# Longer leads in a hand-written issue order, a recurrence split into three chains, and a triangular inverse begun on 16x16 blocks

## The chip, the cores and the metric

One core of one Trainium2 chip runs the whole program. The metric is the time of one execution in microseconds (us). The kernel before took 1440.12, 1442.78 and 1443.78 us in three runs, so its median is 1442.78 us. The trace is of one further execution, which took 1445.36 us.

The engines are PE (TensorE, matrix products), DVE (VectorE), ACT (ScalarE), POOL (GpSimd) and SP (SyncE, which here only starts DMAs). PEld is the loading of weights into TensorE.

## What is computed

A transformer block on 512 tokens of width 1024: an input projection, differential attention with 8 heads, a gated delta rule with 8 key heads and 16 value heads, a gated merge, an MLP and a gated last branch. What matters here is the gated delta rule and the end of attention:

```
lower = tril(einsum(k_beta, k) * decay, -1)            # one 64x64 block per chunk and head
tmat  = triangular_solve(eye + lower, eye, lower=True, unit_diagonal=True)
u, w  = tmat @ v_beta, tmat @ (k_beta * exp(gc))
for each chunk:                                        # state is carried from chunk to chunk
    v_new = u_c - w_c @ state
    o_c   = (q_c * exp(gc)) @ state + intra_c @ v_new
    state = state * exp(g_last) + k_dec.T @ v_new
o_b = rmsnorm(o, gain) * silu(z)

w = softmax(s)                                         # attention, two softmaxes a head
o = rmsnorm((w[0] - lam * w[1]) @ v, gain)
```

Both kernels use chunks of 128 instead of 64, which is the same function. So each of the 8 key heads has 8 matrices of 128x128 to invert (2 value heads by 4 chunks).

## The kernel before

The program is one list of work for five engines. In the part that the change touches, the *mix stage*, PE runs two kinds of work. The *filler* is the input projection: 88 tiles, each of 24 matmuls of 128x512, whose weights arrive through SP (`raw<-w`, line 104), are split by ACT (113, 114) into a high part `whi` and a low part `wlo`, and completed by a DMA that POOL starts (115). The *chains* are the small dependent steps of a head: `gdn_a` (products of keys and queries, line 392), `gdn_i` (the inverse, 480), `gdn_b` (the rest of the delta rule, 504) and `attn` (650).

A planner writes PE's order while the program is built (lines 311 to 355). Each chain is a generator. Its `yield r` says that its next step may be put into the list when PE has been given r more microseconds of work, counted by a fixed price per matmul. Steps that are due go first; between them filler matmuls go in, two at a time. So `yield` sets how much filler lies between a PE step and the next step, which needs what DVE, ACT or a DMA makes of the first. If the number is smaller than what the other engines take, PE waits there, since PE and all other engines run their lists in order. The order on the other engines is set by the framework's scheduler from the same program.

The inverse is made in blocks. `gdn_i` writes the 32x32 diagonal blocks of `B` to DRAM (`ld_d`, line 462) and loads them back so that each of 128 partitions holds one matrix and a quarter of the columns (`L`, 486). DVE substitutes forward in 31 steps of two instructions (494, 495) into `Uq`. Four DMAs write `Uq` to DRAM (`ud_d`, 499) and four bring it back as the diagonal blocks of `U` (502). Then `gdn_b` transposes the blocks on DVE (512 to 514) and joins 32 to 64 and 64 to 128 by matmuls into `psY`, `psT`, `psU`, `ps6` and `ps7`. After that come the four chunks of the recurrence (550 to 605), the norm of the result on DVE (608 to 611), and its transposition into `psoT` (617). All of `gdn_b` of a head waits for `gdn_b` of the head before and for its gate tiles (line 737).

The lines that the prediction's steps touch most:

```
511   yield 8.0          # from the issue of the loads of U to the transposes
516   yield 3.0          # from the transposes to psY
612   yield 6.0          # from the norm of o to psoT
683   yield 5.0 + 0.5 * b    # from the weights of the softmax to psaT
702   yield 5.0          # from the norm of attention's output to psaoT
```

Of the kernel before, what the change touches and what calls it, by code (L numbers as in the profile page):

```python
# [17 lines left out]
T = 512  # L18
# [9 lines left out]
C_W = C_IDT + 256  # L28
# [8 lines left out]
def hybrid_block(ctx, tc, xT, pT, w1, wba, wa, wb, wo, wup, wdn, wple, wpg, vecs, rows, consts, out):  # L37
# [28 lines left out]
    idT = C[:, C_IDT:C_IDT + 256]  # L66
# [215 lines left out]
    ld_d = dram.tile([8, 32, 1024], F32, name="ld_d")  # L282
# [8 lines left out]
    Y6 = bp.tile([128, 8, 64], F32, name="Y6")  # L291
    Ubuf = [bp.tile([128, 8, 128], F32, name=f"U{i}") for i in range(2)]
    for t in (TT, TA, Yx, Y6, *Ubuf):
        G.memset(t, 0.0)

# [96 lines left out]
    def gdn_a(hk):  # L392
# [67 lines left out]
        for b in range(4):  # L460
            dst = ld_d[hk].rearrange("(e b) (r n) -> r b e n", b=4, r=32)[:, b]
            nc.sync.dma_start(dst, Bf[32 * b:32 * b + 32, :, 32 * b:32 * b + 32])
# [17 lines left out]
    def gdn_i(hk):  # L480
# [3 lines left out]
        L = gpool.tile([128, 32, 32], F32, name="L")  # L484
        for q in range(4):
            nc.sync.dma_start(L[32 * q:32 * q + 32].rearrange("p r n -> p (r n)"), ld_d[hk])
        Uq = gpool.tile([128, 8, 32], F32, name="Uq")
        tmp = gpool.tile([128, 256], F32, name="tmpq")
        V.tensor_copy(Uq.rearrange("p m r -> p (m r)"), idT)
        yield 8.0  # L490
        for j in range(31):
            m, r = j // 4 + 1, 31 - j
# [5 lines left out]
        for q in range(4):  # L498
            nc.sync.dma_start(ud_d[hk].rearrange("p (m q) n -> p q m n", q=4)[:, q], Uq[32 * q:32 * q + 32])  # L499
# [4 lines left out]
    def gdn_b(hk):  # L504

        d = st_.pop(hk)
        (kqh, kql), kt, vb, B, intra, U, r2, eq, edr = (d[n] for n in ("kqs", "kt", "vb", "B", "intra", "U", "r2", "eq", "edr"))
        Bf = B.rearrange("p i c n -> p (i c) n")
        U4 = U.rearrange("p e (k n) -> p e k n", k=4)
        b0, b1, b2, b3 = (slice(32 * i, 32 * i + 32) for i in range(4))  # L510
        yield 8.0
# [4 lines left out]
        yield 3.0  # L516
# [30 lines left out]
        o = [bp.tile([128, NC, 128], F32, name=f"o{i}") for i in range(2)]  # L547
        sso = bp.tile([128, 2, NC], F32, name="sso")
# [57 lines left out]

        rt = bp.tile([128, 2, NC], F32, name="rt")
# [4 lines left out]
        yield 6.0  # L612
# [37 lines left out]
    def attn(h):  # L650
# [9 lines left out]
        sso = apool.tile([128, NC], F32, name="asso")  # L660
        yield 1.5
        for b in range(NC):
# [15 lines left out]
            rr = apool.tile([128, 2], F32, name="rr", bufs=3)  # L678
            V.reciprocal(rr, st[:, 2:4])
# [37 lines left out]
    def units():  # L717
        for h in range(-1, 8):
            if h >= 0:
                yield gate_tile(h, 0)  # L720
                yield gate_tile(h, 1)
            if h == 7:
                for n in range(16):
                    yield branch_gate(n)
# [324 lines left out]
```

## Time and profile before

| | |
|---|---|
| the profiled execution | 1445.36 us, of which the span of the trace is 1443.4 us |
| median of three runs | 1442.78 us |
| PE busy | 1351.0 us, 94% of the span |
| DVE, ACT, POOL busy | 825.5, 655.1, 213.3 us |
| PE busy from 200 to 680 us | 439.00 of 480 us |
| PE busy from 800 us to the end | 617.61 of 643.4 us |

The mix stage lies from about 40 to 800 us. From 200 to 680 us the same pattern repeats once a head, about every 85 us. A matmul of 128x512 starts every 0.23 us when TensorE's granted clock is 1.00 (2.4 GHz) and every 0.43 us when it is 0.50 (1.2 GHz). A matmul in plain float32 of the small kind shows as two records in the trace, and as one row in the lists of instructions. "Idle" before an instruction is the time for which its engine had nothing to do, with what released it.

### The profile page before, as it was taken

The page shows a single profiled execution, that of the slowest core. Times are in us where ns is not written, and L with a number is a line of the kernel's source. Part 1 is how long each engine was busy: PE and PEld are TensorE (multiplying, and loading weights), DVE is VectorE, ACT ScalarE, POOL GpSimd, SP SyncE. Part 2 cuts the span into 40 slices and gives each one's busy share as a digit, 9 for nine tenths or more (in the row PEclk, how much of TensorE's full clock was granted, in tenths as well). Part 3 has the DMA queues.
Part 4 walks back from the last instruction along what each step waited for, and adds up shares of the span by engine and source line. Part 5 has one row for each costly group of instructions (what it writes and reads, how often), then busy time and mean ns, then how long its engine had stood idle before and what let it go on. Part 6 is the DMA issues. An engine that isn't in the chain of part 4 may idle for free.

```text
span 1443.4 us, 20586 instructions
## 1 busy us (share of the span) xinstructions
PE 1351.0 (94%) x7378; PEld 1104.5 (77%) x7378; DVE 825.5 (57%) x2324; ACT 655.1 (45%) x1322; POOL 213.3 (15%) x230
## 2 busy tenths in 40 slices
PE   6999999989998999898999999999999999999985
PEld 4777777868776777776877878888888888888985
DVE  6559585867958587694732353357443224433574
ACT  5656565655555565464645332254332223223241
POOL 3221111111111111111001000000421001210241
PEclk9999999999999999999999999999999999999998
DMA  7877656565565665656597863352123233233321
GB/s 233 192 185 171 142 137 148 149 154 139 142 144 124 154 147 140 146 125 133 142 243 191 234 220 117 116 167 83 49 91 97 93 92 98 89 102 102 110 81 59
DMA packets 93879, 197.73 MB, mean 137 GB/s; under 512 B 33713, under 2 KB 39217, under 8 KB 93777
## 3 DMA queue, kind: packets, MB, share of 16 engines
q1 hardware_dynamic: 81104, 150.28, 34.3%
q0 software_dynamic: 12672, 46.14, 17.0%
q8 instruction: 58, 0.95, 0.3%
q14 instruction: 45, 0.36, 0.1%
HBM read 133.40 MB, written 16.84 MB: 104 GB/s over the span
## 4 chain that ended last, share of the span: by engine, by line
PE 62%; DVE 17%; DMA 10%; issue 2%; ACT 2%; SPq 1%; POOL 0%; ACTq 0%; POOLq 0%; DVEq 0%
PE ps L78 52%; DVE acc L362 3%; DMA U<-ud_d 2%; PE psat L78 2%; DMA wlo<-raw 2%; DMA ud_d<-Uq 2%; DVE Uq L495 2%; DVE tmpq L494 1%; DMA ot<-ob_d 1%; DMA g_d<-gth 1%; DVE h L830 1%; PE psS L78 1%; SPq L499 1%; DVE ht L829 1%; PE psx L78 1%
## 5 line engine op out<-in xcount | busy, mean ns | idle before, releaser
L78 PE MATMUL ps<-u_hi,whi 128*128 128x512 f32 (+1 forms) x952 | 389.5, 410 | 1.0 <-DVE mr L889 1.0
L78 PE MATMUL ps<-u_lo,whi 128*128 128x512 f32 (+1 forms) x952 | 375.5, 395 | 0.0
L78 PE MATMUL ps<-u_hi,wlo 128*128 128x512 f32 (+1 forms) x952 | 254.0, 405 | 3.2 <-DMA wlo<-raw 3.2
L78 PEld LDWEIGHTS ps<-u_hi,whi 128*128 128x128 f32 x952 | 182.5, 192 | 41.9 <-issue 3.4
L78 PEld LDWEIGHTS ps<-u_hi,wlo 128*128 128x128 f32 x952 | 180.0, 195 | 44.0 <-DMA wlo<-raw 4.4
L78 PEld LDWEIGHTS ps<-u_lo,whi 128*128 128x128 f32 x952 | 181.8, 191 | 35.1
L96 ACT CAST whi<-raw 128x1024 fp32r<-128x1024 f32 (+1 forms) x93 | 92.3, 994 | 225.8 <-PE ps L78 220.1
L97 DVE TENSOR_TENSOR wlo<-raw,whi 128x1024 fp32r<-128x1024 f32 x83 | 101.2, 1220 | 108.0 <-PE ps L78 87.5
L115 POOL DMA_DIRECT2D wlo<-raw x88 | 76.2, 866 | 569.9 <-ACT wlo L114 368.0
L113 ACT CAST whi<-raw 128x1024 fp32r<-128x1024 f32 x88 | 92.1, 1046 | 80.1 <-PE ps L78 78.2
L114 ACT ACTIVATE wlo<-whi 128x1024 fp32r<-128x1024 f32 x88 | 92.6, 1052 | 0.0
L78 PE MATMUL ps<-hid_lo,whi 128*128 128x512 f32 x224 | 88.6, 395 | 0.0
L78 PE MATMUL ps<-hid_hi,whi 128*128 128x512 f32 x224 | 88.5, 395 | 0.0
L78 PE MATMUL ps<-brh,whi 128*128 128x512 f32 x208 | 82.4, 397 | 0.7 <-ACT whi L96 0.7
L78 PE MATMUL ps<-brl,whi 128*128 128x512 f32 x208 | 82.3, 396 | 0.0
L362 DVE SCALAR_TENSOR_TENSOR acc<-ps,cw,acc 128x511 f32<-128x511 f32 (+2 forms) x96 | 71.5, 744 | 12.3 <-ACT acc L359 11.9
L891 POOL TENSOR_TENSOR mr<-mr 128x512 f32<-128x512 f32 (+1 forms) x37 | 39.3, 1064 | 218.5 <-ACT hid_hi L890 218.4
L889 DVE SCALAR_TENSOR_TENSOR mr<-ps,r 128x512 f32<-128x512 f32 (+1 forms) x37 | 22.9, 619 | 74.1 <-PE ps L78 70.6
L78 PE MATMUL ps<-hid_hi,wlo 128*128 128x512 f32 x224 | 56.8, 395 | 0.0
L495 DVE TENSOR_TENSOR Uq<-Uq,tmpq 128x60 f32<-128x60 f32 (+24 forms) x248 | 52.4, 211 | 4.0
L494 DVE TENSOR_TENSOR tmpq<-L,Uq 128x60 f32<-128x60 f32 (+24 forms) x248 | 51.5, 207 | 3.4
L78 PE MATMUL ps<-brh,wlo 128*128 128x512 f32 x208 | 52.9, 396 | 0.0
(317 smaller groups left out, 2377.2 us busy)
## 6 DMA issues: line engine op xcount, KB each, us to landing
raw<-w SPq DMA_DIRECT2D x88, 512.0 KB, 3.8
wlo<-raw POOLq DMA_DIRECT2D x88, 512.0 KB, 5.3
raw<-wup SPq DMA_DIRECT2D x32, 512.0 KB, 3.5
raw<-wdn SPq DMA_DIRECT2D x32, 512.0 KB, 3.6
raw<-wb SPq DMA_DIRECT2D x16, 512.0 KB, 4.0
gB<-gcr_d SPq DMA_DIRECT2D x16, 256.0 KB, 4.2
bB<-ber_d SPq DMA_DIRECT2D x16, 256.0 KB, 4.8
L<-ld_d SPq DMA_DIRECT2D x32, 128.0 KB, 4.8
```

Of the source, the lines that this page charges most:

```text
L78: PE.matmul(ps, lhsT=lhsT, rhs=rhs, start=start, stop=stop, **k)
L96: S.copy(hi, src)
L97: (eng or V).tensor_tensor(lo, src, hi.bitcast(F32), op=sub)
L113: S.copy(whi, raw)
L114: S.activation(wlo, whi.bitcast(F32), AF.Copy, scale=-1.0)
L115: nc.gpsimd.dma_start(wlo, raw, accum_op=add)
L362: V.scalar_tensor_tensor(acc[:, s:], in0=ps[:, :T - s], scalar=cw[:, j, w:w + 1], in1=acc[:, s:], op0=mult, op1=add)
L494: V.tensor_tensor(tv, bc(L[:, j, j + 1:], [128, m, r], 1), bc(Uq[:, :m, j], [128, m, r], 2), op=mult)
L495: V.tensor_tensor(Uq[:, :m, j + 1:], Uq[:, :m, j + 1:], tv, op=sub)
L499: nc.sync.dma_start(ud_d[hk].rearrange("p (m q) n -> p q m n", q=4)[:, q], Uq[32 * q:32 * q + 32])
L889: V.scalar_tensor_tensor(r[:, :n], in0=ps[:, :n], scalar=0.0, in1=r2[:, sl], op0=mx, op1=mult)
L891: G.tensor_tensor(r[:, :n], r[:, :n], r[:, :n], op=mult)
```

## The change

The change does these things:

- The diagonal blocks that DVE inverts are 16x16. `ld_d` is written by 8 DMAs, `L` is loaded by 2 of 64 partitions, and the substitution has 15 steps of two instructions. A new first part of the chain joins 16 to 32 with two groups of 32 matmuls, `psY16` and `psU16`, which use all four groups of 32 columns in turn. It needs a transpose of each of the four 32-row groups of `U`, four scalings and four copies.
- `gdn_b` is split into `gdn_u` (inverse), `gdn_s` (recurrence) and `gdn_n` (norm and `psoT`), so that the three can be in different heads at once; only `gdn_n` waits for the gate tiles.
- Several leads are longer: 12.0 and 5.0 where 8.0 and 3.0 stood, 11.0 for 6.0 ahead of `psoT`, 6.0 + 0.5 b for 5.0 + 0.5 b ahead of `psaT`, 7.0 for 5.0 ahead of `psaoT`.
- Attention keeps its two softmaxes unnormalized and folds their sums into one factor and into the epsilon of the norm: one long DVE instruction a block goes, short ones on one column come.
- The filler's order in a head is key, query, values, then attention's three tiles, then the gates of the head before.
- Two DMAs fill `ud_d` with zeros at the start, since only its 16x16 blocks are written later.

```diff
...
-    ld_d = dram.tile([8, 32, 1024], F32, name="ld_d")
+    ld_d = dram.tile([8, 64, 256], F32, name="ld_d")
...
+    T3 = bp.tile([128, 8, 32], F32, name="T3")
+    Ye = bp.tile([128, 8, 2, 16], F32, name="Ye")
...
-    for t in (TT, TA, Yx, Y6, *Ubuf):
+    for t in (TT, TA, Yx, Y6, T3, Ye, *Ubuf):
...
+    for i in range(2):
+        nc.sync.dma_start(ud_d[4 * i:4 * i + 4].rearrange("h (p b) j n -> h p (b j n)", p=32).rearrange("h p n -> (h p) n"), Ubuf[i].rearrange("p e n -> p (e n)"))
...
-        for b in range(4):
-            dst = ld_d[hk].rearrange("(e b) (r n) -> r b e n", b=4, r=32)[:, b]
-            nc.sync.dma_start(dst, Bf[32 * b:32 * b + 32, :, 32 * b:32 * b + 32])
+        for b in range(8):
+            bs = slice(16 * b, 16 * b + 16)
+            dst = ld_d[hk].rearrange("(s e b) (r n) -> s b r e n", s=2, b=4, r=16)[b % 2, b // 2]
+            nc.sync.dma_start(dst, Bf[bs, :, bs])
...
-        L = gpool.tile([128, 32, 32], F32, name="L")
-        for q in range(4):
-            nc.sync.dma_start(L[32 * q:32 * q + 32].rearrange("p r n -> p (r n)"), ld_d[hk])
-        Uq = gpool.tile([128, 8, 32], F32, name="Uq")
-        tmp = gpool.tile([128, 256], F32, name="tmpq")
+        L = gpool.tile([128, 16, 16], F32, name="L")
+        for q in range(2):
+            nc.sync.dma_start(L[64 * q:64 * q + 64].rearrange("p r n -> p (r n)"), ld_d[hk])
+        Uq = gpool.tile([128, 8, 16], F32, name="Uq")
+        tmp = gpool.tile([128, 128], F32, name="tmpq")
...
-        for j in range(31):
-            m, r = j // 4 + 1, 31 - j
+        for j in range(15):
+            m, r = j // 2 + 1, 15 - j
...
-        for q in range(4):
-            nc.sync.dma_start(ud_d[hk].rearrange("p (m q) n -> p q m n", q=4)[:, q], Uq[32 * q:32 * q + 32])
+        for q in range(2):
+            for i in range(2):
+                h16, p = slice(16 * i, 16 * i + 16), 64 * q + 32 * i
+                nc.sync.dma_start(ud_d[hk][:, h16, h16].rearrange("p (m q) n -> p q m n", q=2)[:, q], Uq[p:p + 32])
...
-    def gdn_b(hk):
...
-        d = st_.pop(hk)
-        (kqh, kql), kt, vb, B, intra, U, r2, eq, edr = (d[n] for n in ("kqs", "kt", "vb", "B", "intra", "U", "r2", "eq", "edr"))
+    def gdn_u(hk):
...
+        B, U = (st_[hk][n] for n in "BU")
...
-        b0, b1, b2, b3 = (slice(32 * i, 32 * i + 32) for i in range(4))
-        yield 8.0
+        bq = b0, b1, b2, b3 = [slice(32 * i, 32 * i + 32) for i in range(4)]
+        yield 12.0
...
+        T16 = [TT[:, :, 0], TA[:, :, 1], TT[:, :, 1], T3]
+        for i in range(4):
+            V.transpose(T16[i][bq[i]], U4[bq[i], :, i])
+        Y16 = [Ye[:, :, 0], Yx[:, :, 0, :16], Ye[:, :, 1], Yx[:, :, 1, :16]]
+        yield 5.0
+        psY16 = pb.tile([128, 8, 16], F32, name="psY16", tag="b")
+        for e in range(8):
+            for i in range(4):
+                mm(psY16[bq[i], e], Bf[:, e, bq[i]], T16[i][:, e, :16])
+        for i in range(4):
+            if i % 2:
+                S.activation(Y16[i][bq[i]], psY16[bq[i]], AF.Copy, scale=nm16[bq[i]])
+            else:
+                V.tensor_scalar(Y16[i][bq[i]], psY16[bq[i]], nm16[bq[i]], None, op0=mult)
+        yield 2.0
+        psU16 = pb.tile([128, 8, 16], F32, name="psU16", tag="b")
+        for e in range(8):
+            for i in range(4):
+                mm(psU16[32 * i:32 * i + 16, e], Y16[i][:, e], U4[:, e, i, 16:])
+        for i in range(4):
+            (S.copy if i % 2 else V.tensor_copy)(U4[32 * i:32 * i + 16, :, i, 16:], psU16[32 * i:32 * i + 16])
+        yield 2.0
...
-        yield 3.0
+        yield 5.0
...
-        o = [bp.tile([128, NC, 128], F32, name=f"o{i}") for i in range(2)]
-        sso = bp.tile([128, 2, NC], F32, name="sso")
+    def gdn_s(hk):
...
+        d = st_[hk]
+        (kqh, kql), kt, vb, intra, U, r2, edr = (d[n] for n in ("kqs", "kt", "vb", "intra", "U", "r2", "edr"))
+        o = d["o"] = [bp.tile([128, NC, 128], F32, name=f"o{i}") for i in range(2)]
+        sso = d["sso"] = bp.tile([128, 2, NC], F32, name="sso")
...
+    def gdn_n(hk):
...
+        d = st_.pop(hk)
+        o, sso, eq = (d[n] for n in ("o", "sso", "eq"))
...
-        yield 6.0
+        yield 11.0
...
+        l2 = apool.tile([128, NC], F32, name="l2")
...
-            rr = apool.tile([128, 2], F32, name="rr", bufs=3)
-            V.reciprocal(rr, st[:, 2:4])
-            V.tensor_tensor(rr[:, 1:2], rr[:, 1:2], nlam, op=mult)
-            V.tensor_scalar(ws[1][:, :n], ws[1][:, :n], rr[:, 1:2], None, op0=mult)
-            V.scalar_tensor_tensor(ws[0][:, :n], in0=ws[0][:, :n], scalar=rr[:, 0:1], in1=ws[1][:, :n], op0=mult, op1=add)
-            yield 5.0 + 0.5 * b
...
+            rr = apool.tile([128, 1], F32, name="rr", bufs=3)
+            V.reciprocal(rr, st[:, 3:4])
+            V.scalar_tensor_tensor(rr, in0=rr, scalar=st[:, 2:3], in1=nlam, op0=mult, op1=mult)
+            V.tensor_scalar(l2[:, b:b + 1], st[:, 2:3], st[:, 2:3], EPS, op0=mult, op1=mult)
+            V.scalar_tensor_tensor(ws[0][:, :n], in0=ws[1][:, :n], scalar=rr, in1=ws[0][:, :n], op0=mult, op1=add)
+            yield 6.0 + 0.5 * b
...
-        V.tensor_scalar(sso, sso, 1.0 / 128.0, EPS, op0=mult, op1=add)
+        V.scalar_tensor_tensor(sso, in0=sso, scalar=1.0 / 128.0, in1=l2, op0=mult, op1=add)
...
-        yield 5.0
+        yield 7.0
...
     def units():
...
-            if h >= 0:
-                yield gate_tile(h, 0)
-                yield gate_tile(h, 1)
-            if h == 7:
-                for n in range(16):
-                    yield branch_gate(n)
-            else:
-                yield aq_tile(h + 1)
+            if h < 7:
...
+                yield aq_tile(h + 1)
...
-    done |= {(n, -1) for n in ("kq_read", "B_read", "k_read", "av_read", "B", "T", "A", "I")}
+            if h >= 0:
+                yield gate_tile(h, 0)
+                yield gate_tile(h, 1)
+        for n in range(16):
+            yield branch_gate(n)
...
+    done |= {(n, -1) for n in ("kq_read", "B_read", "k_read", "av_read", "B", "T", "A", "I", "U")}
...
-        chains.append([0.0, (("I", h), ("B", h - 1), ("Z", h, 1)), gdn_b, h, ("B", h)])
+        chains.append([0.0, (("Z", h, 1), ("S", h)), gdn_n, h, ("B", h)])
+        chains.append([0.0, (("U", h), ("B", h - 1)), gdn_s, h, ("S", h)])
+        chains.append([0.0, (("I", h), ("U", h - 1)), gdn_u, h, ("U", h)])
...
+    c[:, C_NM] = np.where(p % 32 >= 16, -1.0, 0.0)
```

On PE, at the place where the inverse of head 4 (counted from 0) reaches PE. Before, the last filler matmuls, then `psY` (the first join, 32x32), then attention's `psav`:

```order
L78 MATMUL ps<-u_hi,whi_5242 128x512
L78 MATMUL ps<-u_lo,whi_5242 128x512
L78 MATMUL psY<-TT,B 32x32 x16
L78 MATMUL psav<-C,vT 128x128 x4
L78 MATMUL ps<-u_hi,whi_5242 128x512
L78 MATMUL ps<-u_lo,whi_5242 128x512
```

Now, at the same place of the same head, `psY16` begins (its name is printed without the digits of the tile):

```order
L80 MATMUL ps<-u_hi,whi_5295 128x512
L80 MATMUL ps<-u_lo,whi_5295 128x512
L80 MATMUL psY_5363<-TT,B 32x16
L80 MATMUL psY_5363<-TA,B 32x16
L80 MATMUL psY_5363<-TT,B 32x16
L80 MATMUL psY_5363<-T_346,B 32x16
```

What stood as one block of 16 rows, two groups of columns in turn, now has 32 rows of four groups in turn ahead of it, with half the columns; `psU16` (32 rows of 16x16) follows 10 filler matmuls later, and the old `psY` after that.

On DVE, ahead of the instructions that normalize `o` (the inputs of `psoT`). Before, in head 3:

```order
L494 TENSOR_TENSOR tmpq<-L,Uq 128x75
L90 TENSOR_TENSOR nw_t<-rt 128x8
L698 TENSOR_SCALAR asso<-asso 128x4
L495 TENSOR_TENSOR Uq<-Uq,tmpq 128x5x15
L91 TENSOR_TENSOR nw_t<-nw_t,nw_h 128x8
L87 TENSOR_SCALAR art<-asso 128x4
L494 TENSOR_TENSOR tmpq<-L,Uq 128x70
L92 SCALAR_TENSOR_TENSOR rt<-nw_t,rt 128x8
L88 TENSOR_SCALAR nw_h<-asso 128x4
L495 TENSOR_TENSOR Uq<-Uq,tmpq 128x5x14
L611 TENSOR_TENSOR o_4545<-o_4545,rt 128x512
L611 TENSOR_TENSOR o_4546<-o_4546,rt 128x512
```

Now, in head 3:

```order
L94 SCALAR_TENSOR_TENSOR rt<-nw_t,rt 128x8
L92 TENSOR_TENSOR nw_t<-art 128x4
L92 TENSOR_TENSOR nw_t<-rt 128x8
L93 TENSOR_TENSOR nw_t<-nw_t,nw_h 128x4
L93 TENSOR_TENSOR nw_t<-nw_t,nw_h 128x8
L94 SCALAR_TENSOR_TENSOR art<-nw_t,art 128x4
L94 SCALAR_TENSOR_TENSOR rt<-nw_t,rt 128x8
L92 TENSOR_TENSOR nw_t<-art 128x4
L651 TENSOR_TENSOR o_4736<-o_4736,rt 128x512
L651 TENSOR_TENSOR o_4737<-o_4737,rt 128x512
```

The steps of the substitution (`tmpq`, `Uq`), which stood between the steps of the norm, are gone from here; only attention's norm (`art`) still alternates with it.

On SP, around the way of the inverse through DRAM. Before, in head 2:

```order
L104 DMA raw_3403<-w 128x1024
L499 DMA ud_d<-Uq 256x1x32 x4
L104 DMA raw_3552<-w 128x1024
L502 DMA U_346<-ud_d 32x8x32 x4
L104 DMA raw_3712<-w 128x1024
L104 DMA raw_3819<-w 128x1024
```

Now, in head 2:

```order
L106 DMA raw_3365<-w 128x1024
L509 DMA ud_d<-Uq 32x8x16 x4
L512 DMA U_348<-ud_d 32x8x32 x4
L106 DMA raw_3480<-w 128x1024
L750 DMA oa_d<-of 128x512
```

The load of weights that stood between the writes of `ud_d` and the loads of `U` now stands behind both in five of the eight heads, as here.

## Rows read from the trace of the kernel before

**Rows 1.** The page: span, then busy time of PE and DVE with share and instructions.
```profile
span 1443.4 us, 20586 instructions
PE 1351.0 (94%) x7378; PEld 1104.5 (77%) x7378; DVE 825.5 (57%) x2324; ACT 655.1 (45%) x1322; POOL 213.3 (15%) x230
```

**Rows 2.** Stretches (us): length, busy PE, PEld, DVE, ACT, POOL, PEclk (granted clock), DMA.
```profile
200.00:680.00 480.00, 439.00 (x2649) 350.89 (x2647) 342.39 (x1219) 271.68 (x635) 71.14 (x78) 0.96 0.60 141
680.00:800.00 120.00, 113.02 (x648) 91.70 (x649) 55.05 (x203) 64.44 (x134) 12.92 (x15) 1.00 0.73 186
800.00:1443.40 643.40, 617.61 (x3166) 520.67 (x3164) 293.84 (x500) 197.08 (x300) 84.65 (x83) 0.98 0.35 111
```

**Rows 3.** What PE waited for: total us, times, longest us.
```profile
PE psoT L78 <- DVE o L611: 19.5, 6, 3.3
PE psY L78 <- DVE TT L513: 14.2, 6, 2.6
PE psaT L78 <- DVE aw L682: 6.2, 8, 1.4
PE psY L78 <- DVE TT L512: 2.0, 3, 1.0
PE psaoT L78 <- DVE oo L701: 1.6, 1, 1.6
PE psaT L78 <- DVE Uq L495: 1.5, 1, 1.5
```

**Rows 4.** PE in order of time: start, us, operation, count, [idle before <- releaser].
```profile
378.74 1.94 PE L78 MATMUL psoT<-C,o 128*128 128x128 f32 x8 [3.25 <-DVE o L611]
```

**Rows 5.** The stretch behind that wait, columns as in rows 2.
```profile
378.50:384.50 6.00, 5.76 (x18) 4.92 (x19) 4.64 (x22) 1.04 (x1) 0.00 (x0) 0.50 0.49 174
```

**Rows 6.** DVE in order of time ahead of that psoT.
```profile
377.92 1.28 DVE L611 TENSOR_TENSOR o<-o,rt 128x512 f32<-128x512 f32 x2
```

**Rows 7.** The inverse's way to PE in head 6, on DVE.
```profile
651.59 0.16 DVE L495 TENSOR_TENSOR Uq<-Uq,tmpq 128x8 f32<-128x8 f32 x1
...
666.05 0.44 DVE L513 STREAM_TRANSPOSE TT<-U 32x256 f32<-32x256 f32 x1
```

**Rows 8.** The same on SP.
```profile
652.25 4.70 SPq L499 DMA_DIRECT2D ud_d<-Uq  x4
659.28 2.94 SPq L502 DMA_DIRECT2D U<-ud_d  x4
```

**Rows 9.** The same on PE.
```profile
663.76 0.22 PE L78 MATMUL psY<-TT,B 128*32 128x32 f32 x2 [1.04 <-DVE TT L512]
666.54 0.69 PE L78 MATMUL psY<-TT,B 128*32 128x32 f32 x30 [2.56 <-DVE TT L513]
```

**Rows 10.** PE around psY in head 0, where nothing was late.
```profile
149.55 0.39 PE L78 MATMUL ps<-u_lo,whi 128*128 128x512 f32 x1
149.88 0.70 PE L78 MATMUL psY<-TT,B 128*32 128x32 f32 x32
150.50 0.33 PE L78 MATMUL psav<-C,vT 128*128 128x128 f32 x1
```

**Rows 11.** psT (one group of columns) and ps6 (64 columns), as rows 10.
```profile
152.96 0.60 PE L78 MATMUL psT<-Yx,U 128*32 128x32 f32 x13
...
157.31 1.15 PE L78 MATMUL ps<-TA,B 128*64 128x64 f32 x16
```

**Rows 12.** Groups by line: engine, operation, shape, count, busy us, mean ns, idle before.
```profile
L495 DVE TENSOR_TENSOR Uq<-Uq,tmpq 128x60 f32<-128x60 f32 (+24 forms) x248 | 52.4, 211 | 4.0
L681 DVE TENSOR_SCALAR aw<-aw,rr 128x128 f32<-128x128 f32 (+3 forms) x32 | 12.2, 380 | 0.1
L113 ACT CAST whi<-raw 128x1024 fp32r<-128x1024 f32 x88 | 92.1, 1046 | 80.1 <-PE ps L78 78.2 <-DMA raw<-w 1.4
```

**Rows 13.** SP in order of time at the start.
```profile
25.27 1.03 SPq L104 DMA_DIRECT2D raw<-w  x2
33.18 0.32 SPq L196 DMA_DIRECT2D pp_d<-pp  x1
```

More of the change, by code (lines that the diff above doesn't have):

```diff
@@ L27 @@
 C_ID, C_TRI, C_MJI, C_MQK, C_IDT = (128 * i for i in range(5))
-C_W = C_IDT + 256
+C_NM = C_IDT + 128
+C_W = C_NM + 1
 G_MIX, G_PMIX, G_MLP, G_PMLP, G_PLE = (8 * i for i in range(5))
@@ L65, in hybrid_block @@
     mqk = C[:, C_MQK:C_MQK + 128]
-    idT = C[:, C_IDT:C_IDT + 256]
+    idT = C[:, C_IDT:C_IDT + 128]
+    nm16 = C[:, C_NM:C_NM + 1]
     def bc(ap, shape, axis):
@@ L992, in _constants @@
     c[:, C_MQK:C_MQK + 128] = np.where(col <= row, 0.0, NEG)
-    m, i = np.arange(8)[None, :, None], np.arange(32)[None, None, :]
-    c[:, C_IDT:C_IDT + 256] = (i == 4 * m + p[:, None, None] // 32).reshape(128, 256)
+    m, i = np.arange(8)[None, :, None], np.arange(16)[None, None, :]
+    c[:, C_IDT:C_IDT + 128] = (i == 2 * m + p[:, None, None] // 64).reshape(128, 128)
+    c[:, C_NM] = np.where(p % 32 >= 16, -1.0, 0.0)
     return c
```

## The prediction

> **What bounds the kernel now.** I read the page first. PE is busy 1351 of 1443.4 us, DVE 825.5 [rows 1]: PE's work is the bound, and only PE's waits, its slow clock and its own work can move the end. Next the table by stretches, to find where PE loses time. From 200 to 680 us it is idle for 480 − 439 = 41 us and the granted clock is 0.96, while DVE and ACT have plenty of room (342 and 272 of 480); from 680 to 800 us PE is idle 7 us; behind 800 us the change touches nothing [rows 2]. Third, the list of PE's waits names the causes: `psoT` for the normalized `o`, 19.5 us; `psY` for the transposed inverse, 14.2 + 2.0; `psaT` for attention's weights, 6.2 + 1.5; `psaoT`, 1.6 [rows 3]. That is 45.0 us, nearly all of it in the mix stage. Filler matmuls stand behind each of these instructions in PE's list and cannot pass them. Fourth, the timeline shows a second price: `psoT` starts after 3.25 us of idleness [rows 4], and the 6 us from there have a granted clock of 0.50, that is 1.2 GHz [rows 5]. Everything in such a stretch takes about twice as long.
>
> **What goes.** (a) The waits. At `psoT` the lead of 6.0 was 3.25 us too short [rows 4], so about 9.3 is needed; 11.0 is given, and the substitution's steps no longer stand among the norm's on DVE. At `psY` in the worst head, 6, the lead of 8.0 + 3.0 was short by 1.04 + 2.56 [rows 9], so 14.6 is needed from the issue of the loads. That agrees with the rows: the last step of `Uq` ends at 651.75, SP issues the four writes from 652.25 to 656.95 and the four loads from 659.28 to 662.22, and the second of the transposes that `psY` needs most ends at 666.49, 14.7 us after `Uq` [rows 7, 8]. Now 12.0 + 5.0 = 17.0 is given. `psY16` needs the fourth block of `U` too, which was not on this path: one more transpose of 0.44 and perhaps 0.5 for its landing, 15.7. A margin of 1.3 us in the worst head remains. At `psaT` the longest waits were 1.4 and 1.5, and the other seven take 4.8 together, 0.7 each [rows 3]; the lead grows by 1.0, and the instruction of line 681, 380 ns in the mean, goes from the path [rows 12]. At `psaoT` it is 2.0 against 1.6. So I let all 45.0 go and charge for what comes back under (d).
>
> (b) The slow clock. 480 us at a mean of 0.96 is 19 us lost [rows 2]. A part of each slow stretch lies in the idle time itself, which (a) has counted: in the 6 us after the wait this is 0.24 [rows 5]. I take 17 us. It goes only where the idle time ahead of it goes.
>
> **What comes.** (c) PE's own work. Each head gets 32 matmuls `psY16` and 32 `psU16`, 64 records each. No row shows a matmul of 16 columns or four groups of columns in turn. The nearest is the old `psY`: 32 records in two groups in turn hold PE from 149.88 to 150.50, 0.62 us or 19 ns each, and its start is 0.33 us behind the matmul ahead instead of 0.23 [rows 10]; the change back costs about as much. At this pace a group costs 64 × 0.0194 + 0.2 = 1.44 us, and 16 groups 23 us. From below: if four groups in turn go twice as fast as two did, or 16 columns twice as fast as 32, 64 × 0.0097 + 0.2 = 0.82, 13 us. From above: `psT` stays in one group and takes 0.60 for 13 records, 0.52 without the overlap that `psY` shows at its end, 40 ns each [rows 11]; that gives 2.8 us, 44 us for 16. Nothing hides this work, since PE is the bound. I take 22, the nearest row.
>
> The row says that a record of 32 columns can start every 19 ns. The Trainium skill (TensorE: Matmul & The Clock Gate, "Seeing it yourself") says that the distance from start to start never falls below about 25 ns, however small the matmul. This speaks against the change: by it, half the columns save nothing, an estimate of 64 × 0.025 + 0.2 = 1.8 us a group and 29 us for 16, and the sum below would be 1418 instead of 1411. The trace does not bear it out at 32 columns; nothing here shows 16.
>
> (d) New waits. The chain gets two more turns between engines. `psY16` to `psU16` has 2.0 for two scalings on DVE and two on ACT; the old `psY` to `psT` had the same lead with one on each, and PE's wait for it does not stand among the larger ones [rows 3]. `psU16` to `psY` has 2.0 + 5.0, for two copies and three transposes, well covered. `psaoT` now comes close to `psoT`, and attention's norm stands behind the two long instructions of `o` on DVE (1.28 us [rows 6]). I charge 5 us for the eight heads, from 0 to 15.
>
> (e) The start. The second load of filler weights was issued at 25.3 us and the last write of `pp_d` at 33.2 [rows 13]; now SP holds that load until behind this write, and fills `ud_d` with 1 MB of zeros ahead of the first. I charge 3 us, from 0 to 7.
>
> **What costs or gives nothing.** The substitution had 248 pairs of about 0.21 us each [rows 12] and has 120 smaller ones; with line 681 DVE loses some 65 us of work and gets some 25 back in transposes, scalings and copies. DVE is idle 138 us of these 480 [rows 2], so this is worth only what it does to the waits in (a). On SP `ld_d` takes 8 issues instead of 4, `L` 2 instead of 4. In five heads SP now issues the writes of `ud_d` and the loads of `U`, 652.25 to 662.22 [rows 8], with no load of weights between them. ACT's reading of `raw` waited 78.2 us for PE and 1.4 for the load itself [rows 12], so loads come early and this is hidden; without that cover it would be the 2.9 us of the loads of `U` [rows 8] in each of five heads. Splitting `gdn_b` in three lets the next inverse begin beside the recurrence, but filler lies between the steps everywhere, so the split alone shortens nothing: it makes room for the longer leads.
>
> **The sum**, against the profiled execution's 1445.4 us: −45 − 17 + 22 + 5 + 3 = −32, so 1413. That execution was 2.6 us above the median of the runs, 1442.8; from the median it is **1411 us**.
>
> **The rivals.**
> - *Four groups run side by side.* (c) falls to 13 us and (d), (e) to about 3: −62 + 16 = −46, 1397 us. For it: two groups in turn took half of what one group takes (19 and 40 ns). Against it: nothing shows that PE issues faster than one record in 19 ns.
> - *The waits move instead of going.* If half of (a) and (b) stays, because the fourth block of `U` lands later or because `psU16` and `psaoT` wait, −31 + 22 + 5 + 3 = −1, 1442 us: no change, and the leads do not do what they are for. For it: the margin of 1.3 us at `psY16` is thin, and DVE keeps its list in order. Against it: each lead grows by more than its wait was long.
> - *Narrow matmuls cost more than the waits: slower.* `ps6`, with 64 columns, takes 1.15 us for 16 records, 72 ns each [rows 11]. If a record of `psY16` or `psU16` costs that, because its weights are loaded with nothing to hide them, a group costs 64 × 0.072 + 0.2 = 4.8 us and 16 cost 77: −62 + 77 + 8 = +23, 1466 us. The point from which this decides is (62 − 8) / 16 = 3.4 us a group, 50 ns a record. For it: 16 columns give a weight load little to hide behind. Against it: `psY` at 19 ns also loaded weights for each matmul.
>
> **Chances.** My forecast 0.63; four groups side by side 0.13; waits that move 0.15, of which 0.04 end faster, 0.08 the same and 0.03 slower; narrow matmuls 0.05, and 0.04 for a slower end that I do not name. A change within 0.3%, 4.3 us, cannot be told from none. So faster 0.80, same 0.08, slower 0.12. The range, from (c) to (e) at their lower and upper ends: −62 + 13 gives 1394; the upper end takes (c) at 40 ns with (d) and (e) as charged, −62 + 44 + 8 = −10, 1433. Beyond it lie most of the moved waits and the slower cases, below it little, so about 2 in 10 is outside: 1394 to 1433.
>
> **What would show it.** In the list of PE's waits `psoT`, `psaT` and `psaoT` fall below 1 us a head and `psY` leaves the list; the granted clock from 200 to 680 us is 0.99 or more. A `psY16` group holds PE for 1.2 to 1.7 us until the next filler matmul. The head's period falls from 85 us to about 82. The stretch behind the mix stage keeps its 643 us. I am wrong if PE waits more than 1 us a head for the transposes of `psY16`, if a group holds PE for more than 3 us, or if PE waits for `wlo<-raw` in the heads where SP stands before `U`.

## The result and the profile after

The changed kernel took 1418.5, 1422.03, 1422.86 and 1429.2 us, median **1422.4 us**, beside 1442.7 for the kernel before: a ratio of 0.9865, 95% interval 0.9835 to 0.9896. Run again later beside other kernels it gave 1421.7 us and 0.9865 [0.9838, 0.9893]. So it is 20 us faster; 1411 was forecast, in a range of 1394 to 1433. The profiled execution is the one of 1418.5 us.

The page of the changed kernel, as [rows 1]:

```profile
span 1416.7 us, 22558 instructions
PE 1343.1 (95%) x8402; PEld 1101.9 (78%) x8402; DVE 801.6 (57%) x2132; ACT 665.0 (47%) x1354; POOL 213.6 (15%) x232
```

PE has 1024 records more and is busy 8 us less. Next stretches of the changed kernel, as [rows 2] but with PE alone (length, busy PE, granted clock, DMA share, GB/s):

```profile
200.00:660.00 460.00, 443.93 (x3483) 0.99 0.60 144
660.00:780.00 120.00, 113.48 (x754) 0.96 0.73 187
790.80:1416.70 625.90, 599.53 (x3105) 0.99 0.34 109
```

In the stretch of the repeated pattern PE is idle 16 us of 460 instead of 41 of 480, at a clock of 0.99 instead of 0.96. The tail of the mix stage got worse: 0.96 instead of 1.00. The last row begins at the first matmul of the next stage (`brh`); in the kernel before this was at 813.1 us and the rest took 630.3 us. So of the 26.7 us between the two spans 22.3 lie in the mix stage and 4.4 behind it. The change touches nothing there, and that rest took 625.2 to 635.2 us in the kernels of the experiments.

What PE waited for in the mix stage of the changed kernel, as [rows 3]:

```profile
PE psU L80 <- ACT Yx L533: 5.5, 2, 3.6
PE ps L80 <- DMA wlo<-raw: 4.3, 3, 2.0
PE psN L80 <- DVE vs L613: 3.9, 4, 1.7
PE psaoT L80 <- DVE eq L478: 3.8, 1, 3.8
PE psat L80 <- POOL k L681: 3.4, 5, 1.6
PE psao L80 <- ACT aT L730: 3.2, 3, 2.2
PE psaT L80 <- DVE aw L724: 1.1, 1, 1.1
```

`psoT` and `psY` are gone, `psaT` fell from 7.7 to 1.1, `psaoT` rose to 5.3 in three waits, of which 3.8 is shown. The rest is new or larger. Two of these waits cost most, since the clock falls behind them. (It falls to 0.66 behind two shorter ones too, `psao` at 98.5 us and a `psN` at 418.5.) The first is in head 7, where `psU16` waits for the scalings of `psY16`. DVE, then ACT, then PE of the changed kernel:

```profile
704.55 0.34 DVE L535 TENSOR_SCALAR Ye<-psY,C 32x128 f32<-32x128 f32 x1 [3.38 <-PE psY L80]
710.35 1.23 DVE L99 TENSOR_TENSOR brl<-ot,brh 128x1024 fp32r<-128x1024 f32 x1 [5.46 <-ACT brh L98]
711.61 0.35 DVE L535 TENSOR_SCALAR Ye<-psY,C 32x128 f32<-32x128 f32 x1
```
```profile
709.28 1.04 ACT L98 CAST brh<-ot 128x1024 fp32r<-128x1024 f32 x1 [3.79 <-DMA ot<-oa_d]
710.35 0.36 ACT L533 ACTIVATE Yx<-psY,C 32x128 f32<-32x128 f32 x1
```
```profile
710.76 0.23 PE L80 MATMUL psU<-U,Yx 128*16 128x16 f32 x2 [3.63 <-ACT Yx L533]
712.01 0.24 PE L80 MATMUL psU<-U,Ye 128*16 128x16 f32 x2 [1.02 <-DVE Ye L535]
714.12 0.21 PE L80 MATMUL psU<-U,Yx 128*16 128x16 f32 x1 [1.86 <-ACT Yx L533]
```

Read from the bottom: PE waits for a scaling on ACT; it stands behind a cast that belongs to the next stage, and that cast waits for its load `ot`. DVE is caught in the same way between its two scalings. The stretch around it in the changed kernel:

```profile
700.00:710.00 10.00, 7.13 (x93) 0.97 1.01 337
710.00:720.00 10.00, 6.35 (x75) 0.51 0.78 184
```

The DMA share was 1.01 in the ten microseconds ahead, in which the load was under way, and the clock is 0.51, so 1.2 GHz nearly throughout, behind it. The second wait, `psaoT` at 535 us, DVE and then PE:

```profile
530.08 0.43 DVE L524 STREAM_TRANSPOSE TT<-U 32x256 f32<-32x256 f32 x1 [1.03 <-DMA U<-ud_d]
...
534.14 0.69 DVE L743 TENSOR_TENSOR oo<-oo,art 128x512 f32<-128x512 f32 x1
```
```profile
534.98 0.70 PE L80 MATMUL psaoT<-C,oo 128*128 128x128 f32 x4 [3.81 <-DVE eq L478]
```

The last multiplication of attention's norm stands on DVE behind the transposes of `U`. These wait for their loads, but only 1.2 us of the 3.8 (1.03, and 0.20 at the second transpose). For the rest DVE works through its list: it is busy 4.47 of the 5 us (PE, PEld, DVE, ACT and POOL, then clock and DMA as above):

```profile
530.00:535.00 5.00, 1.19 (x6) 0.65 (x5) 4.47 (x19) 2.38 (x7) 0.86 (x1) 1.00 0.72 177
```

The other new waits are shorter and mostly of this second kind. The longest `psN`, DVE and then PE:

```profile
185.28 0.74 DVE L369 SCALAR_TENSOR_TENSOR acc<-ps,cw,acc 128x509 f32<-128x509 f32 x1
185.94 0.60 DVE L724 SCALAR_TENSOR_TENSOR aw<-aw,rr 128x384 f32<-128x384 f32 x1
186.46 0.34 DVE L613 TENSOR_SCALAR vs<-psV,edr 128x128 f32<-128x128 f32 x1
```
```profile
186.95 0.67 PE L80 MATMUL psN<-vs,kt 128*128 128x256 f32 x2 [1.75 <-DVE vs L613]
```

Its input `vs` stands behind a step of a later tile's convolution (`acc`) and behind attention's weights (`aw`), and DVE waits for nothing there.

PE around a `psY16` group of the changed kernel:

```profile
298.99 0.39 PE L80 MATMUL ps<-u_lo,whi 128*128 128x512 f32 x1
299.31 0.20 PE L80 MATMUL psY<-TT,B 128*32 128x16 f32 x1
...
299.86 0.18 PE L80 MATMUL psY<-T,B 128*32 128x16 f32 x1
299.97 0.50 PE L80 MATMUL ps<-u_hi,whi 128*128 128x512 f32 x1
```

These 64 records (32 float32 matmuls) hold PE for 0.66 us, and the first starts 0.32 behind the matmul ahead instead of 0.23.

### The profile page after: what moved, and what is told of

The parts are those of the page before. It is cut to its first block, busy times and chain, and to the rows that moved or that the text cites. A ratio compares the mean times of both kernels' runs of the same rounds, so it can differ in the third digit from the quotient of the medians.

```text
span 1416.7 us, 22558 instructions
## 1 busy us (share of the span) xinstructions
PE 1343.1 (95%) x8402; PEld 1101.9 (78%) x8402; DVE 801.6 (57%) x2132; ACT 665.0 (47%) x1354; POOL 213.6 (15%) x232
## 4 chain that ended last, share of the span: by engine, by line
PE 50%; DVE 5%; DMA 4%; ACT 1%; issue 1%; POOL 0%; SPq 0%; ACTq 0%; POOLq 0%; DVEq 0%
PE ps L80 45%; DMA ot<-ob_d 1%; DMA g_d<-gth 1%; DMA wlo<-raw 1%; DVE h L873 1%; DVE ht L872 1%; PE psat L80 1%; PE psS L80 0%; PE psO L80 0%; PE psV L80 0%; DVE ss L859 0%; PE psr L153 0%; PE psao L80 0%; PE pss L145 0%; DVE nw_t L93 0%
## 5 line engine op out<-in xcount | busy, mean ns | idle before, releaser
L80 PE MATMUL ps<-u_hi,whi 128*128 128x512 f32 (+1 forms) x952 | 384.3, 405 | 0.3 <-DVE mr L932 0.3
L80 PE MATMUL ps<-u_lo,whi 128*128 128x512 f32 (+1 forms) x952 | 371.5, 391 | 0.0
L80 PE MATMUL ps<-u_hi,wlo 128*128 128x512 f32 (+1 forms) x952 | 250.1, 396 | 4.3 <-DMA wlo<-raw 4.3
L80 PEld LDWEIGHTS ps<-u_hi,wlo 128*128 128x128 f32 x952 | 173.0, 190 | 40.2 <-DMA wlo<-raw 5.5
L80 PEld LDWEIGHTS ps<-hid_lo,whi 128*128 128x128 f32 x224 | 42.1, 188 | 10.3
L80 PEld LDWEIGHTS ps<-hid_hi,wlo 128*128 128x128 f32 x224 | 42.0, 188 | 10.3
```

Source lines behind the costliest of these rows:

```text
L80: PE.matmul(ps, lhsT=lhsT, rhs=rhs, start=start, stop=stop, **k)
```

## The experiments

Two theories stood at the start. *Leads*: the longer leads earn the gain and the 16-row inverse only costs. *Room*: the leads fit only because the inverse is shorter and the chains are split. Where the cost of the clock is told below, it is the sum of (1 − granted clock) over the stretches of 5 us from 60 us to the end of the mix stage: 22.2 us in the kernel before, 10.2 in the changed one.

**1. The kernel before with the longer leads alone.**

```
511  yield 8.0  -> 12.0      516  yield 3.0 -> 5.0      612  yield 6.0 -> 11.0
683  yield 5.0 + 0.5 * b -> 6.0 + 0.5 * b               702  yield 5.0 -> 7.0
```

> The kernel before with the longer leads alone (12 and 5 ahead of psY, 11 ahead of psoT, 6 + 0.5 b and 7 in attention); one gdn_b chain, the 32-row inverse and the old units stay. Theory: the leads earn the whole gain. The 42 us of waits at psoT, psY and psaT leave the list and 13 us of slow clock go with them: 1443 - 55 = 1388, plus up to 10 of new waits, so 1388 to 1400. Rival: in one chain the longer leads leave too little filler for head 7, whose last two recurrence steps and norm then have none behind them: two steps of 3 to 4 us, 9 us at the last psoT, and as much again at half clock, 20 to 30 us: 1408 to 1420, with the new waits at the end of the mix stage.

1431.5 us, ratio 0.9917 [0.9888, 0.9946]. Both ends missed. The waits named did go (`psoT` 0.2 us in all), but these stand in their place:

```profile
PE psat L78 <- POOL k L641: 9.0, 11, 1.8
PE ps L78 <- DMA wlo<-raw: 7.3, 3, 3.7
```

They are mostly not at the end of the stage, as the rival said, but at attention's steps (`psat` 21.3 us in all, from the first head on). The clock still costs 20.4 us. So the leads alone are worth 11 to 12 of the 20 us.

**2. The changed kernel with the inverse on 32-row blocks again.** Removed: the fill of `ud_d`, `psY16`, `psU16`; back: 31 substitution steps. Leads, three chains, units and folded sums stay.

> The changed kernel with the inverse on 32-row blocks again (31 substitution steps; no psY16, no psU16, no fill of ud_d); three chains, longer leads, folded sums and the new order of units stay. Theory: the 16-row inverse only costs (about 12 us of its matmuls, 2 at the start, 6.5 us of waits at psU16 in head 7 and their slow clock): 1422 - 24 = 1398, from 1394 to 1404. Rival: the shorter substitution is what makes room for the leads in a head's period; without it filler ends before head 7 does and 15 to 25 us of waits come at the end of the mix stage: 1413 to 1428.

1430.8 us, 0.9908 [0.9874, 0.9941]. The theory (1394 to 1404) falls: without the 16-row inverse the kernel is 6 to 8 us *slower* (by the ratios and by the medians), though PE has 1024 records fewer. The rival gave the sign, an upper end 3 us too low, and the place only in part (three waits from 731 to 759 us, 7.8 us in all):

```profile
PE psx L78 <- DVE intra L455: 8.5, 4, 2.1
PE ps L78 <- DMA wlo<-raw: 7.5, 4, 4.9
```

`psx` waits 2.1 us in four heads for an instruction on DVE, and the clock falls behind each, to 0.66 in the next 5 us. In the stage PE is idle 8.8 us longer than in the changed kernel and the clock costs 10.3 us more, 20.5 in all; together that is more than the 12 us of narrow matmuls that went. Right ahead of `intra` on DVE stand a later tile's convolution and attention's weights, and no step of the substitution. So that DVE's longer list brings the wait about is likely, and not shown.

**3. The changed kernel with all old leads** (12 → 8, 5 → 3 ahead of `psY16`, 11 → 6, 6 → 5, 7 → 5).

> The changed kernel with the old leads (8 and 3 ahead of psY16, 6 ahead of psoT, 5 + 0.5 b and 5 in attention); all else stays. Theory: the waits return, 3.2 us at psoT and 3 to 4.5 us at psY16 a head, with their slow clock: 1422 + 45 = 1467, from 1455 to 1480. Rival: the shorter lists of DVE (substitution halved, sums folded) make the old leads long enough, and at most 1 us a head comes back: 1422 to 1435.

1440.9 us, 0.998 [0.9956, 1.0005]: between the two, 17 to 19 us slower than with the leads (by the ratios and by the medians). `psY16` waited in no head. `psoT` waited 7.0 us in three, not 19.5 in six. PE's idle time in the stage is 13 us longer in all, much of it in attention (`psat` for `k` 8.3 us, for `oo` 5.3), and the clock costs 23.8 us.

**4. The changed kernel with the narrow groups issued twice.**

```
-        for e in range(8):             # psY16, and the same for psU16
+        for e in [*range(8)] * 2:
```

> The changed kernel with each of the 16 groups of 64 narrow records (psY16 and psU16) issued twice into the same place, so 1024 records more. By the trace of the changed kernel a record starts 8 ns after the one ahead: +0.55 us a group, +9 us, 1431. As forecast (19.4 ns): +20 us, 1442. By the Trainium skill's floor of about 25 ns from start to start (TensorE: Matmul & The Clock Gate, Seeing it yourself), an estimate: +26 us, 1448.

1447.4 us, 1.0024 [1.0, 1.0047], so +23 to +25 us. By the total the floor of the Trainium skill looks right; the trace says otherwise. A `psY16` group of 128 records holds PE for 1.20 us instead of 0.66: 0.54 us for 64 records more, 8.4 ns each. `psU16` groups without a stall take 1.16 to 1.31. That makes 9 us for 16 groups. The rest is mostly stalls for which the profile names no cause ("issue"):

```profile
234.14 0.19 PE L80 MATMUL psU<-U,Yx 128*16 128x16 f32 x1 [2.90 <-issue]
```

There are seven, 11.4 us in all, against one of 0.7 in the changed kernel. The run confirms the pace of the records, but it doesn't price a group of 64, since that group stalls hardly anywhere.

**5 to 7. Longer leads where the new waits are.** Run 5: `psU16` of head 7 stands 10.0 behind `psY16`. Run 6: the lead of `psaoT` goes from 7.0 to 11.0. Run 7: both, and 2.5 instead of 2.0 ahead of `psN`.

```
+        yield 2.0 if hk < 7 else 10.0     # 5 and 7: ahead of psU16
+        yield 11.0                        # 6 and 7: ahead of psaoT
+            yield 2.5                     # 7: ahead of psN and psO
```

> The changed kernel with one lead longer: psU16 of head 7 stands 10.0 instead of 2.0 behind psY16. Theory: in the changed kernel the scalings of psY16 stand on DVE and ACT behind the next stage's splits of ot, which wait for their loads, and psU16 then costs 6.5 us of waits and 4.9 us of slow clock (0.50 and 0.53 in the 10 us from 710). With filler ahead of it both go: 1422 - 11 = 1411, from 1408 to 1415. Rival: the delay moves, since the chain of head 7 ends later and the last psoT has no filler left ahead of it, or the clock falls there: 1418 to 1426.

> The changed kernel with the lead of psaoT at 11.0 instead of 7.0. Theory: the 3.8 us at 535 come from DVE's list: oo's norm stands behind the transposes of the next U, which wait for their loads. Filler of 4 us covers it: 3.8 + 0.8 + 0.7 us of waits and 1.7 us of slow clock (0.66 in 5 us) go: 1422 - 7 = 1415, from 1412 to 1418. Rival: the order on DVE shifts with it and the same wait comes at another head or instruction: 1420 to 1426.

> The changed kernel with both leads above and 2.5 instead of 2.0 ahead of psN and psO in the recurrence. Theory: the parts add, 11 + 7, and 2 to 4 of the 5.5 us at psN: 1422 - 21 = 1401, from 1397 to 1408. Rival: the last psoT of head 7 now stands behind the last filler, so up to 9 us and its slow clock come back at the end of the stage: 1410 to 1420.

Run 5: 1421.1 us, 0.9833 [0.9803, 0.9863], so the rival's time, but not by its cause, an end of the stage without filler. `psU16` no longer waits, but a filler weight comes late in the same place, behind ten microseconds in which the DMA share is 1.00. Run 5, the stretch and then PE:

```profile
703.00:713.00 10.00, 10.00 (x106) 1.00 1.00 329
```
```profile
717.21 1.22 PE L80 MATMUL ps<-u_hi,wlo 128*128 128x512 f32 x2 [3.68 <-DMA wlo<-raw]
```

So a wait of 3.7 us for a weight stands where 6.5 us for the scalings stood. That full DMA queues hold this weight up is likely, and not shown. Run 6: 1415.8 us, 0.9795 [0.9768, 0.9821], as the theory said. `psaoT` waits at most 0.9 us. Run 7: 1418.1 us, 0.9821 [0.9788, 0.9853]; the parts don't add. In five heads `psO` and `psV` now wait 0.7 to 1.3 us each, where the changed kernel had 2.4 us in all, while `psN` fell from 5.5 to 0.8. Why these waits moved from one to the other is open.

**8. The kernel before with the 16-row inverse alone** (old leads, one chain, old units, old attention).

> The kernel before with the 16-row inverse alone: its substitution of 15 steps, psY16, psU16 and the fill of ud_d; one chain, leads of 8, 3 and 6, the old attention and the old units stay. Theory: it costs its PE work (16 groups of 0.75 us, 12 us, and 2 at the start), but the waits at psY (16 us and 4 to 5 of slow clock) go with it, since in the run with old leads its writes to ud_d landed after 1.6 us instead of 4.9 and psY16 waited nowhere; psoT keeps its 19.5: 1442 - 21 + 14 = 1435, from 1430 to 1440. Rival: with leads of 11 in all psY16 waits as psY did, and the inverse is a pure cost: 1452 to 1460. Third: it removes the waits at psoT too: 1412 to 1425.

1444.6 us, 0.9999 [0.9977, 1.0021]: no change, and no theory hit it. The waits at `psY` went, as the first theory said. The round trip through DRAM shortened; the lines on the writes and the loads of `ud_d` from 200 to 680 us, first the kernel before, then run 8:

```profile
L499 SPq DMA_DIRECT2D ud_d<-Uq x24: 567/602/1745, 221.9 to 655.3; - x24
DMA to landing us min/median/max: 3.4/5.3/6.0
...
L502 SPq DMA_DIRECT2D U<-ud_d x24: 337/442/1548, 228.6 to 660.7; - x24
DMA to landing us min/median/max: 3.4/5.1/5.9
```
```profile
L509 SPq DMA_DIRECT2D ud_d<-Uq x20: 318/450/2167, 276.5 to 619.1; - x20
DMA to landing us min/median/max: 1.5/3.1/5.5
...
L512 SPq DMA_DIRECT2D U<-ud_d x20: 303/442/651, 282.1 to 625.3; - x20
DMA to landing us min/median/max: 1.7/2.8/5.6
```

In the medians 4.5 us are saved, and 3.6 were missing in the worst head [rows 9]. But these 4.5 us are the smaller part of it. The last step of the substitution and the start of `psY16` in head 6 of run 8, as rows 7 and 9:

```profile
617.18 0.18 DVE L503 TENSOR_TENSOR Uq<-Uq,tmpq 128x8 f32<-128x8 f32 x1
```
```profile
641.92 0.20 PE L80 MATMUL psY<-TT,B 128*32 128x16 f32 x1
```

That is 25 us, and 25 to 31 in heads 1 to 6; in the kernel before it is 12 us, and 11 to 12. Half as many steps end earlier, and the chain then starts behind the head before: `psY16` comes 12 to 15 us after the last `psoT`, where `psY` came after 21 to 24. The loads of `U` landed 12 to 22 us ahead of `psY16`, so by these figures the waits at `psY` would have gone without the shorter way through DRAM.

`psoT` fell from 19.5 to 8.2 us with the old lead. But `psaT` rose from 7.7 to 13.3, `psU` waits 7 us, PE has its 12 us of narrow matmuls, and its first filler matmul comes 3.7 us later. PE's idle time in the stage hardly changes, 53.3 us against 54.6. What the inverse saves, it gives away there, at the old leads of attention most of all.

```profile
PE psaT L80 <- DVE aw L727: 9.7, 7, 2.8
PE psoT L80 <- DVE o L651: 8.2, 5, 2.7
```

**9. The version that the runs point to**: both leads of runs 5 and 6, and the fill of `ud_d` moved from the start into head 0's inverse.

```
+        if hk == 0:
+            for i in range(2):
+                nc.sync.dma_start(ud_d[4 * i:4 * i + 4]..., Ubuf[i]...)
         Bf = B.rearrange("p i c n -> p (i c) n")
```

> The changed kernel with psaoT's lead at 11.0, psU16 of head 7 10.0 behind psY16, and the fill of ud_d issued in head 0's inverse instead of at the start. Theory: the run with psaoT's lead, 1416, still had 2.4 us at psU16 in head 7 and 1.7 us of slow clock there, and the fill delays the first use of the filler's weights by 2 us: 1416 - 6 = 1410, from 1406 to 1413. Rival: the late weights (wlo<-raw, 3.7 us in the run with psU16's lead alone) take the place of the wait, and the start is set by other loads: 1414 to 1420.

1411.4 us, 0.979 [0.9761, 0.9819], the theory's: faster than both kernels. Its stretches:

```profile
200.00:660.00 460.00, 448.90 (x3516) 1.00 0.61 145
660.00:779.30 119.30, 113.87 (x762) 1.00 0.76 197
```

The clock costs 1.7 us in the whole stage. The first filler matmul is at 29.7 us instead of 33.9. `wlo<-raw` takes 9.3 us of waits here, 4.3 in the changed kernel, so the rival is there too and is outweighed.

**10. The changed kernel with the lead of `psoT` alone back at 6.0.**

> The changed kernel with the lead of psoT back at 6.0, all else as it is. Theory: the wait at psoT returns in six heads with 2 to 3.3 us and the clock falls behind each (2.4 us each in the kernel before): 12 to 20 and 10 to 14, 1422 + 28 = 1450, from 1444 to 1456. Rival: since the substitution's steps no longer stand among the norm's on DVE, six waits are not there, three of 2.3 us as in the run with all old leads: 1422 + 7 + 6 = 1435, from 1430 to 1440. Third: no change, 1420 to 1426.

1426.1 us, 0.9893 [0.9865, 0.9921]: +4 us, hardly to be told from none, below the rival and far from the theory. Of the 19.5 us of the kernel before, 13.7 stay away with the old lead too. What comes back is hidden in part, since `psaoT` waits 3.8 us less than in the changed kernel; `psU16` in head 7 waits 2.6 us more.

```profile
PE psoT L80 <- DVE o L651: 5.8, 3, 2.6
```

**11. The changed kernel in one chain** (`gdn_u`, `gdn_s`, `gdn_n` of a head one after the other).

> The changed kernel with gdn_u, gdn_s and gdn_n of a head run one after the other as one chain, as gdn_b was; leads, inverse, attention and units stay. Theory: the split makes room for the leads. In one chain the inverse of head 7 comes so late that filler ends after the first step of its recurrence; three steps of about 7 us and a norm of 9 us then stand bare: 1422 + 30 = 1452, from 1442 to 1462. Rival: the split does nothing, since filler lies between the steps everywhere: 1419 to 1427.

1509.9 us, 1.0471 [1.0441, 1.0501]: the theory's sign, three times its size. The chain is late in every head, not in the last alone. The pattern repeats every 96 us, and in each repetition some 30 us pass (364 to 396, for one) in which only two filler matmuls lie between the steps, so every turn stands bare and the clock falls:

```profile
280.00:380.00 100.00, 87.67 (x671) 0.86 0.49 120
```

That is not the work of the leads alone. Run 1 has the same leads in one chain, no stretch in it without filler is longer than 8.3 us, and it took 1431.5 us. Run 11 keeps the new order of the filler, in which a head's gates come last, and one chain starts only behind its own gates. The next value tile of the filler has to wait until `psv` has read the value tile ahead of it, and `psv` comes only when this chain has read `B` for the last time. PE at the end of that stretch in run 11:

```profile
365.03 0.73 PE L80 MATMUL ps<-u_hi,wlo 128*128 128x512 f32 x2
...
396.36 1.06 PE L80 MATMUL psv<-C,vraw 128*128 128x128 f32 x4
397.07 0.78 PE L80 MATMUL ps<-u_hi,whi 128*128 128x512 f32 x1
```

In all six repetitions the filler comes back right behind `psv`. So the run shows that the new order of the filler needs the split.

**12. The changed kernel once more**, as the measure for runs 9 to 11.

> The changed kernel itself, unaltered, beside the three others. Both theories: 1422, from 1418 to 1426, since nothing differs; it is the measure for the others of this set.

1421.7 us.

## Why the prediction was right, and where its terms were not

The time, the sign and the range held. The mechanism holds in kind: waits went and the clock rose with them. In size it holds by half. Of 54.6 us of idle time 40 were to go, and 20.6 went; that the time still lies in the range is in part luck, since two terms missed in opposite directions: (c) measured 10 us less than forecast, below its lower bound of 13, and (d) 13 us more, above its upper bound of 15. The terms, from the traces of the two kernels (the traced executions lie 26.9 us apart, the medians 20):

| term | forecast | measured |
|---|---|---|
| (a) the four waits | −45.0 | −38.6: 45.0 to 6.4, of which `psaoT` 5.3 |
| (b) slow clock | −17 | −12 to −16 |
| (c) narrow matmuls | +22 | +12 |
| (d) new waits | +5 | +18 |
| (e) start | +3 | +2.3 |
| mix stage | −32 | −22.3 |

PE's idle time from the first filler matmul to the end of the stage went from 54.6 to 34.0 us, −20.6; with −38.6 from the four waits, the others grew by 18.0. PE's busy time fell by 4.0 though (c) is in it, which leaves −16.1 for (b), and with this value the terms add up; the sum over the stretches of 5 us gives −12.0. The first filler matmul is at 33.9 instead of 31.6 us.

- **(c) was mis-sized.** It took "the nearest row", 19.4 ns a record with two groups of columns. With four, and half the columns, it is 8.4 ns, the pace of the rival with four groups side by side. 16 × (0.66 + 0.09) is 12 us, below the 13 of the lower bound.
- **(d) was mis-sized, and this is the step that failed**: "I charge 5 us for the eight heads, from 0 to 15". 18 came. The forecast looked at the two new turns of the inverse and at `psaoT` beside `psoT`, and asked of each whether its lead covers its own instructions. It covered them in seven of eight heads at `psU16`. What it didn't ask is what else stands ahead on DVE and ACT. At `psU16` in head 7 it is casts of the next stage's `ot`, which wait for a DMA (704 to 714 us): 6.5 us. In run 5 a longer lead there exchanged the wait for one for a weight. The larger part came at turns whose leads nobody had touched: `psN` and `psV` of the recurrence wait 7.1 us, where it was 0.3, and `psat` and `psao` of attention 7.3, where it was 0.5. At the one that is shown (187 us) DVE is simply busy with other work.
- **`psaoT` is in (a), not in (d)**, and is of the same kind: the transposes of `U` and other work on DVE hold attention's norm (535 us). Run 6 shows it, and its removal brought 6 us by the medians and 10 by the ratios.
- **(a) had nearly the right sum, but not for the reason alone that it gave.** "11.0 is given" stood for `psoT`, beside the steps that left DVE's list there, and 12.0 + 5.0 for `psY`. With the old leads and the new inverse `psY16` doesn't wait (runs 3 and 8), since the shorter substitution ends 15 to 31 us ahead of it in heads 1 to 6, and not 11 to 12 as before, and `psoT` waits 5.8 to 8.2 us instead of 19.5 (runs 3, 8 and 10). With the old inverse and the new leads these waits go too (run 1). Either part removes them, and their prices must not be added.
- **What was costed at nothing was worth something.** The shorter substitution was "worth only what it does to the waits in (a)". Taken back, with all leads in place, the 16-row inverse costs 6 to 8 us (run 2), narrow matmuls and all, by waits that no row of the kernel before shows: `psx` for `intra`, and slow clock behind it.
- **"The split alone shortens nothing: it makes room for the longer leads"** is not shown in either half. No run has the split alone. The leads fit into one chain with the old order of the filler (run 1); what can't do without the split is the new order (run 11, 1510 us).
- Of the two theories of the start neither holds as it stands. The inverse does not only cost (run 2), and the leads alone earn 11 to 12 us in one chain with the old inverse (run 1).
- Of what would show it: `psoT` and `psY` are gone, `psaT` has one wait of 1.1 us, the clock in the repeated part is 0.99. A head's period is 82.2 us (`psY16` at 215.63 and, five heads on, 626.78). No wait for `wlo<-raw` came where SP stands before `U`. But a `psY16` group holds PE for 0.66 us, not 1.2 to 1.7, and `psaoT` has one wait of 3.8.
- *Waits that move* came true for the waits: that rival let half of the 45.0 us stay and charged 5 for new ones, 27.5 in all, and 6.4 + 18.0 = 24.4 us are there. It was wrong on the clock, of which it let 8.5 us go, and it had (c) at 22. So the conditions of two rivals, this one and the four groups side by side, came true together, and they nearly cancel.

The Trainium skill (TensorE: Matmul & The Clock Gate, "Wait — 56ns, not 53.3ns?"; the prediction and run 4 name the section that follows it) says that starts never lie closer than about 25 ns. The rows of the 16-column groups show 0.55 us from the first of 64 records to the last, 8.7 ns each, so for matmuls that go round four groups of columns the measurement decides against the rule.

Left open: how the 18 us divide among the parts of the change, since each edit of a lead moved the planner's order of the others; what the split, the folded sums and the new order of the filler are worth by themselves, since no run takes one of the last two out and run 11 breaks the filler; and the 4.4 us behind the mix stage, which lie within the spread of that stretch.

## What to carry to other kernels

Ask of each wait not only how long its own work takes, but what stands ahead of that work in its engine's list, and whether that in turn waits for a DMA. In these traces the lists run in order, and such a wait is handed to work that has nothing to do with it (5.46 us on DVE at 710 us). Ask it of the turns too that the change leaves alone: they brought more than half of the new waits here. Two parts of a change that remove the same wait must be priced together, and one part alone may show nothing (run 8). A part that looks like one of many may be what another rests on (run 11). A wait on PE may be paid twice, in idle time and in slow clock behind it, but its length does not tell when. In the kernel before, the six `psoT` waits of 3.2 to 3.3 us have a clock of 0.50 to 0.66 in the 5 us behind them in five heads and 1.00 in one; in the changed kernel it is 0.66 behind one of 1.6 us (418.5) and 1.00 behind one of 2.0 (74.7).

## What the runs showed of the hardware

- 64 records of 16 columns (32 float32 matmuls) that go round four groups of columns hold PE for 0.66 us, weight loads included, and 128 hold it for 1.20, 8.4 ns for each one more. With 32 columns, two groups had taken 19 ns a record [rows 10] and one group 40 ns [rows 11]. From two to four groups the columns were halved too, and no run tells the two apart.
- In and shortly behind runs of 128 such records PE stalled seven times, for 0.8 to 2.9 us, with no wait in the profile (run 4). In the changed kernel this is one stall of 0.7 us. Near four of the longest, the queue that carries instructions moved one packet of 16 KB each (in the half microseconds from 231.5, 321.0, 400.5 and 572.0); it moved 74 packets in run 4 and 66 in the changed kernel. The Trainium skill (Runtime: NRT & Kernel Launch, "Instruction fetch mechanics") says that instructions arrive in blocks of 256 by a DMA queue of their own; the 8 packets more for 2048 instructions more, weight loads counted, agree. That the stalls are these fetches is not shown, since unstalled groups have such a packet near them too (489.5 in run 4).
- The same loads of `U`, 32 KB each with the same shape, landed after 5.1 us in the median in the kernel before, after 3.9 in run 1 and after 2.8 in run 8 (200 to 680 us). The writes of `ud_d` landed after 5.3 us (32 KB each), 3.5 (run 1, the same size) and 3.1 (run 8, 16 KB). So the size of the blocks does not account for the difference; what does is open.
